# Dead tiles that hold evacuations and two more raw weight tiles, a quadrant joined by DMA, and a chunk's bank from another pool

## The chip, the cores and the metric

The kernel runs on one core of a Trainium2 chip. The metric is the device time of one execution in microseconds (us). TensorE is called PE, VectorE DVE, ScalarE ACT, GpSimd POOL, and SyncE SP; SP issues most of the weight loads and POOL the transfers that accumulate.

## What is computed

Two layers of a hybrid decoder on 512 tokens of width 1024, in float32, and a last norm:

```python
def hybrid_layer(x, ...):
    h = rmsnorm(x, g_mix)
    z = h @ w_in                       # q, k, v | retention q, k, v, g | two gates
    A = sliding_window_sink_attention(rope(aq), rope(ak), av, sinks) @ w_a
    B = (group_norm(chunkwise_retention(rq, rk, rv)) * silu(rg)) @ w_b
    x = x + (sigmoid(ga) * A + sigmoid(gb) * B) @ w_out
    return x + jnp.square(jax.nn.relu(rmsnorm(x, g_mlp) @ w_up)) @ w_down   # 1024 -> 4096 -> 1024

def reference(x, ...):
    for l in range(2): x = hybrid_layer(x, ...)
    return rmsnorm(x, g_final)
```

## The kernel before, in words

**Precision.** Every float32 product is made of three products of rounded halves: a weight `raw` is rounded by ACT into `hi` (L308), DVE takes the difference `lo` (L309), and `products` issues hi·hi, lo·hi and hi·lo as three matmuls (L354, L355, L356). A matmul has 512 or 256 columns.

**Weights.** They come as 361 units of 128 x 1024 in one order (`order`): per layer 46 of `w_in`, then `w_a`, `w_b`, `w_out`, and those of the MLP. `unit` hands out a unit's `hi` and `lo`; before that it splits up to unit i + SPLIT (3) and loads (`load_until`) up to AHEAD (4) units beyond that. There are 5 `raw` tiles and 4 each of `hi` and `lo`. A `raw` tile is given back when its unit is split, so a load, which SP issues, waits for an earlier unit's `lo` or add.

**The MLP** goes in 8 blocks e of 512 hidden columns. It saves products in the way of Strassen: a block's down part has seven products (`down`, parts 0 to 6 of the units "block") on four quadrants (i, j) of the output, i the half of the features and j the half of the tokens, and for e > 0 the up part is two "pair"s of four units each. Sums of weights are made beforehand by POOL DMAs into DRAM (`sum_steps`) or by DVE on the way: `add_part` (L267) for pair parts 1 and 2, `add_block` (L290) for block parts 2 and 4, which are the sum of two earlier raw tiles and load nothing while e < 7. Pair evacuations (`eu`, L1154, L1157; `z`, L1159, L1172; `mm`, L1152) make relu and the hidden forms, whose rounded halves `r` (L361, L362) PE multiplies with the block's units.

**Joining the output.** Blocks 0 to 6 (`Adding`): ACT copies twelve banks a block to SBUF, scaled (L1276), four `early` ones to temporaries `eu` and eight `put` ones to temporaries `y`, all from one pool of 7 buffers; a POOL DMA adds each to `y` in DRAM (L1278). Block 7 (`Ending`): POOL loads the four quadrants back (L1292), DVE adds the last products onto them (`add`, L1307), and the two `early` products of quadrant (1, 1) go by an ACT copy and an accumulating POOL DMA (L1302, L1303). In layer 0 `turn` then transposes each quadrant on PE (L1334) and DVE adds it to x (L1340); quadrants with i = 0 inside `last_but_one`, those with i = 1 in `carry`, which runs inside the first group of layer 1 (j = 1 first, then 0). `scaled_input` splits x into `xh` (L364) and `xl` (L365). In layer 1 the last norm follows instead: a gain product (L1316), squares on ACT, a scale per token (L1323 and L1326), and the output. Its last block's down part takes four `w_end` units.

**Banks.** `ps_mm` has 5 PSUM banks and `ps_aux` 3. `group` multiplies the first four units of `w_in` on four banks at once (key, value, two query columns); two `chunk`s follow, each with one bank of `ps_mm`. The keys are rotated by DVE from their bank (L570, L571) once the norm's scale is known. In the first part of the MLP in layer 1, `turn_x` transposes x on PE (L1069) for the copy that `Adding` starts from (L1071, L1072); after that x is dead until block 7 loads `y` into it. In layer 0 a tile `late_box[0]` waits for the same purpose.

**Order.** Each engine runs its instructions in the order that a scheduler gives them when the kernel is built; no order is written by hand but that of the calls. A change of pools and buffers therefore also moves instructions. SP and POOL issue their DMAs in order too.

## Time and profile before

| | us |
| --- | --- |
| median of three runs (lowest, highest) | 1501.16 (1500.49, 1502.59) |
| the profiled execution | 1501.42 |
| its span, from the first to the last instruction | 1499.7 |
| PE, DVE, ACT, POOL busy | 1471.8, 1044.3, 940.9, 239.7 |

The profile shows one execution. The groups of instructions give a line, an engine, the tile written and the tiles read, a count, the busy time and the mean length, and how long the engine was idle just before them and for whom. The waits list who waited for whom: total, times, longest. The timeline shows single instructions with start and length, and in brackets the idle time before one. The stretches give, for a piece of the span, the busy time of each engine, the clock that PE was granted (1.00 is full) and the share of the DMA engines' time. "DMA to landing" is the least, the median and the greatest time from the issue of a DMA to its last packet. A matmul's shown length reaches past the start of the next one; spacing between starts is what counts.

### The profile page before, as it was taken

To read this page: it belongs to the slowest core of one execution; us is meant where nothing else is said; L and a number is where in the kernel's file an instruction comes from. 1 tells how busy PE (TensorE), PEld (TensorE's weight loads), DVE (VectorE), ACT (ScalarE), POOL (GpSimd) and SP (SyncE) were. 2 spreads that over 40 slices of the span, in tenths; PEclk is the share of its full clock that TensorE was granted. 3 is DMA by queue.
4 is the path that set the end of the run, shared out by engine and by line. 5 is a ranking of instruction groups with operands and counts; after the bars stand their busy time and mean duration, and the time that the engine had idled before them with its cause. 6 is when DMAs were issued, how large, how long until landed. Compare 5 with 4: busy or idle time off the path is not lost.

```text
span 1499.7 us, 21303 instructions
## 1 busy us (share of the span) xinstructions
PE 1471.8 (98%) x7787; PEld 1265.7 (84%) x7787; DVE 1044.3 (70%) x1589; ACT 940.9 (63%) x1551; POOL 239.7 (16%) x334
## 2 busy tenths in 40 slices
PE   9999999999999999999999999999999999999997
PEld 7888888888889999998778888888888789888885
DVE  6878568654677777776977775677447677777665
ACT  7657355532568888887755563555325778877775
POOL 0101121101002222223001011111000212222230
PEclk9999999999999999999999999999999999999999
DMA  7654997668227888888836579876443488888883
GB/s 257 189 169 113 303 256 185 185 179 223 92 72 220 211 215 218 223 213 230 290 100 182 147 207 273 223 205 155 140 121 110 122 205 213 210 219 211 218 205 126
DMA packets 100472, 286.25 MB, mean 191 GB/s; under 512 B 11664, under 2 KB 11792, under 8 KB 96528
## 3 DMA queue, kind: packets, MB, share of 16 engines
q0 software_dynamic: 38832, 114.31, 36.3%
q1 hardware_dynamic: 60816, 169.27, 33.5%
q8 instruction: 61, 1.00, 0.3%
q10 hardware_dynamic: 720, 1.31, 0.2%
q14 instruction: 43, 0.35, 0.1%
HBM read 231.37 MB, written 113.77 MB: 230 GB/s over the span
## 4 chain that ended last, share of the span: by engine, by line
PE 87%; DMA 6%; ACT 3%; DVE 2%; issue 2%; DVEq 0%; ACTq 0%
PE mm L354 23%; PE mm L355 23%; PE mm L356 23%; DMA raw<-w_down_in 3%; DMA raw<-w_pair_in 2%; PE rv L354 2%; PE rv L356 2%; PE rv L355 2%; PE b L354 2%; PE b L355 2%; PE b L356 2%; DVE lo L309 1%; PE score L705 1%; ACT hi L308 1%; PE pT L670 1%
## 5 line engine op out<-in xcount | busy, mean ns | idle before, releaser
L308 ACT ACTIVATE hi<-raw 128x1024 fp32r<-128x1024 f32 (+1 forms) x363 | 369.8, 1020 | 324.4 <-PE mm L355 195.4
L309 DVE TENSOR_TENSOR lo<-raw,hi 128x1024 fp32r<-128x1024 f32 (+1 forms) x364 | 424.5, 1170 | 201.9 <-ACT hi L308 199.8
L354 PE MATMUL mm<-xh,hi 128*128 128x512 f32 (+1 forms) x1008 | 358.4, 359 | 14.4 <-ACT eu L1154 9.5
L355 PE MATMUL mm<-xl,hi 128*128 128x512 f32 (+1 forms) x1008 | 356.9, 356 | 0.0
L356 PE MATMUL mm<-xh,lo 128*128 128x512 f32 (+1 forms) x1008 | 356.2, 356 | 0.7 <-DVE lo L309 0.7
L354 PE MATMUL mm<-r,hi 128*128 128x256 f32 (+1 forms) x736 | 238.7, 324 | 0.5 <-ACT mm L1152 0.5
L356 PE MATMUL mm<-r,lo 128*128 128x256 f32 (+1 forms) x736 | 238.9, 325 | 0.0
L355 PE MATMUL mm<-r,hi 128*128 128x256 f32 (+1 forms) x736 | 238.8, 324 | 0.0
L354 PEld LDWEIGHTS mm<-xh,hi 128*128 128x128 f32 x1008 | 190.7, 189 | 44.2 <-ACT eu L1154 12.5
L356 PEld LDWEIGHTS mm<-xh,lo 128*128 128x128 f32 x1008 | 190.7, 189 | 26.2 <-DVE lo L309 0.9
L355 PEld LDWEIGHTS mm<-xl,hi 128*128 128x128 f32 x1008 | 191.0, 189 | 25.5 <-DVE xl L365 0.2
L354 PEld LDWEIGHTS mm<-r,hi 128*128 128x128 f32 x736 | 139.8, 190 | 13.7 <-ACT mm L1152 0.7
L355 PEld LDWEIGHTS mm<-r,hi 128*128 128x128 f32 x736 | 139.8, 190 | 13.1
L356 PEld LDWEIGHTS mm<-r,lo 128*128 128x128 f32 x736 | 139.8, 190 | 11.3
L1278 POOL DMA_DIRECT2D y<-eu x56 | 47.3, 851 | 387.7 <-ACT eu L1276 383.4
L1278 POOL DMA_DIRECT2D y<-y x112 | 98.1, 1257 | 66.4 <-DMA y<-eu 35.5
L355 PE MATMUL mm<-lo,r 128*128 128x512 f32 x272 | 104.2, 392 | 0.0
L356 PE MATMUL mm<-hi,r 128*128 128x512 f32 x272 | 100.7, 390 | 0.0
L354 PE MATMUL mm<-hi,r 128*128 128x512 f32 x272 | 97.8, 393 | 0.2
L267 DVE TENSOR_TENSOR raw<-raw 128x512 f32<-128x512 f32 x56 | 38.5, 688 | 67.6 <-DMA raw<-sums_up 54.1
L354 PE MATMUL b<-hi,r 128*128 128x512 f32 x180 | 70.5, 392 | 1.6 <-DVE y L1307 1.6
L355 PE MATMUL b<-lo,r 128*128 128x512 f32 x180 | 70.3, 390 | 0.0
(262 smaller groups left out, 2314.3 us busy)
## 6 DMA issues: line engine op xcount, KB each, us to landing
raw<-w_in_in SPq DMA_DIRECT2D x89, 512.0 KB, 5.5
sums_down<-w_down_in POOLq DMA_DIRECT2D x30, 1024.0 KB, 11.3
y<-y POOLq DMA_DIRECT2D x120, 256.0 KB, 7.9
sums_up<-w_pair_in POOLq DMA_DIRECT2D x56, 512.0 KB, 9.8
raw<-w_down_in SPq DMA_DIRECT2D x45, 512.0 KB, 8.7
raw<-w_pair_in SPq DMA_DIRECT2D x84, 256.0 KB, 4.2
raw<-sums_down SPq DMA_DIRECT2D x30, 512.0 KB, 9.1
y<-eu POOLq DMA_DIRECT2D x58, 256.0 KB, 5.8
```

What stands on the lines that cost most here:

```text
L267: nc.vector.tensor_tensor(raws[i][:, at], last[:, LEFT], last[:, RIGHT], ALU.add)
L308: nc.scalar.activation(hi[:, at], raw[:, at], AF.Copy)
L309: nc.vector.tensor_tensor(lo[:, at], raw[:, at], f32(hi[:, at]), ALU.subtract)
L354: nc.tensor.matmul(ps, ah, bh, start=start and i == 0, stop=False, **more)
L355: nc.tensor.matmul(ps, ah, bl, start=False, stop=False, **more)
L356: nc.tensor.matmul(ps, al, bh, start=False, stop=stop and i == n - 1, **more)
L670: nc.tensor.transpose(pt[:, i * P : (i + 1) * P], sm[:, at : at + P], ident)
L705: nc.tensor.matmul(ps[:, g * w : (g + 1) * w], q_s[g][:, c, at], part[:, keys], start=i == 0, stop=i == 1)
L1278: nc.gpsimd.dma_start(y[:, block, i * T : (i + 1) * T], t, **how)
```

## The change

1. `chunk` takes a pool; the last chunk of query columns in each layer takes its bank from `ps_aux`.
2. In layer 0's block 7 the `put` of quadrant (1, 1) is no longer added by DVE but copied by ACT and added by a POOL DMA, as its `early` products are; `carry` turns j = 0 first.
3. `Adding.put` uses a dead tile every second time: one of x's first four slices in layer 1, one of the waiting tile's in layer 0. There are four of them.
4. In layer 1, after the last `turn_x`, the upper half of x becomes two spare raw tiles, lent to pair and block units up to block 6 (`lent`); loads then run two units further ahead (`load_until`), and `fits` holds a load back while no tile of either kind is free.
5. In the last norm the gain product for i = 1 is joined with its scale into one DVE operation of three operands: four DVE instructions fewer.

```diff
--- before.py
+++ after.py
@@ -50,6 +50,7 @@
 DEEP = 3
 DELAY = 2
 AHEAD = 4
+RAW = 5
 SPLIT = 3
 
 
@@ -166,8 +167,22 @@
 
         return (slice(0, UNIT // 2), slice(UNIT // 2, UNIT)) if i < 3 else (slice(0, UNIT),)
 
-    def raw_tile():
-        return wpool.tile([P, UNIT], F32, tag="raw", name="raw", bufs=5)
+    spare = []
+
+    def lent(i):
+        if order[i][1] not in ("pair", "block") or block_of(order[i]) == N_BLOCK - 1:
+            return []
+        return [t for t in spare if not any(t is r for r in raws.values())]
+
+    def fits(i):
+        if order[i][1] == "block" and order[i][3] in (2, 4) and order[i][2] < N_BLOCK - 1:
+            return True
+        taken = sum(not any(t is r for t in spare) for r in raws.values())
+        return taken < RAW or bool(lent(i))
+
+    def raw_tile(i):
+        got = lent(i)
+        return got[0] if got else wpool.tile([P, UNIT], F32, tag="raw", name="raw", bufs=RAW)
 
     x_next = [1]
 
@@ -177,7 +192,7 @@
         nc.sync.dma_start(x[:, k, :], xT[:, k, :])
 
     def load_until(n):
-        while state["loaded"] < min(n, len(order)):
+        while state["loaded"] < min(n, len(order)) and fits(state["loaded"]):
             i = state["loaded"]
             layer, name, j = order[i][:3]
             if name == "pair":
@@ -185,7 +200,7 @@
             elif name == "block":
                 load_block(i)
             else:
-                raws[i] = raw_tile()
+                raws[i] = raw_tile(i)
                 for at in halves(i):
                     queue = nc.scalar if i == 0 and at.start == 0 else nc.sync
                     source = w_end[j] if name == "w_end" else weights[name][layer, j]
@@ -245,11 +260,14 @@
                 if next(steps[0], DONE) is DONE:
                     steps.pop(0)
 
+    def block_of(unit):
+        return unit[2] // 2 + 1 if unit[1] == "pair" else unit[2]
+
     def load_part(i):
         layer, _, j, part = order[i]
         source, sums = w_pair[layer, j], sums_up[layer][j]
         H = UNIT // 2
-        raws[i] = raw = raw_tile()
+        raws[i] = raw = raw_tile(i)
         if part == 0:
             nc.sync.dma_start(raw[:, LEFT], source[:, :H])
             nc.sync.dma_start(raw[:, RIGHT], sums[:, RIGHT])
@@ -270,7 +288,7 @@
         layer, _, e, part = order[i]
         if part in (2, 4) and e < N_BLOCK - 1:
             return
-        raws[i] = raw = raw_tile()
+        raws[i] = raw = raw_tile(i)
         if part in (2, 4):
             nc.sync.dma_start(raw, sums_last[:, part // 2 - 1, :])
             return
@@ -292,7 +310,7 @@
     def split_until(n):
         while state["split"] < min(n, len(order)):
             i = state["split"]
-            load_until(i + AHEAD)
+            load_until(i + AHEAD + len(spare))
             name, part = order[i][1], order[i][-1]
             if name == "pair":
                 add_part(i)
@@ -385,11 +403,11 @@
         while background:
             advance()
 
-    def chunk(name, layer, moving, evacuate, rate=1.0):
+    def chunk(name, layer, moving, evacuate, rate=1.0, pool=ps_mm):
 
         hi, lo = unit(name, layer)
         n = len(moving)
-        ps = bank(ps_mm, "mm")
+        ps = bank(pool, "mm")
         pairs = [((hi[:, k * P : (k + 1) * P], lo[:, k * P : (k + 1) * P]), moving[k]) for k in range(n)]
         advance(rate)
         products(ps, pairs[: n // 2], True, False)
@@ -650,7 +668,7 @@
             {0: squares, 1: rms_mix.prepare, 2: stats} if layer == 0 else {0: carried.pop(), 2: rms_mix.prepare, 3: stats},
         )
         chunk("w_in", layer, xs, put_q(2))
-        chunk("w_in", layer, xs, put_q(3))
+        chunk("w_in", layer, xs, put_q(3), pool=ps_aux)
         turn_v()
 
         a_t = [slots.four() for _ in range(2)]
@@ -1253,6 +1271,9 @@
                 into.put(1, 0, m, b[m], -1)
             into.end()
 
+        homes = [x[:, n, :] if last else late_box[0][:, n, :] for n in range(4)]
+        own = [0]
+
         class Adding:
 
 
@@ -1269,7 +1290,11 @@
                 self.send(i, j, m, temp("eu"), ps, sign, last or self.e > 0)
 
             def put(self, i, j, m, ps, sign):
-                self.send(i, j, m, temp("y"), ps, sign, last or self.e > 0 or j == 1)
+                self.send(i, j, m, self.home(), ps, sign, last or self.e > 0 or j == 1)
+
+            def home(self):
+                own[0] += 1
+                return homes[own[0] // 2 % 4] if own[0] % 2 else temp("y")
 
             def send(self, i, j, m, t, ps, sign, add):
                 block = 2 * j + m
@@ -1298,9 +1323,12 @@
                 if i == 0:
                     self.add(i, j, m, ps, scale)
                 else:
-                    t = temp("eu")
-                    nc.scalar.activation(t, ps, AF.Copy, scale=scale)
-                    nc.gpsimd.dma_start(self.y[i, j, m], t, accum_op=ALU.add)
+                    self.send(i, j, m, ps, scale)
+
+            def send(self, i, j, m, ps, scale):
+                t = temp("eu")
+                nc.scalar.activation(t, ps, AF.Copy, scale=scale)
+                nc.gpsimd.dma_start(self.y[i, j, m], t, accum_op=ALU.add)
 
             def add(self, i, j, m, ps, scale):
                 v = self.y[i, j, m]
@@ -1308,19 +1336,23 @@
 
             def put(self, i, j, m, ps, sign):
                 block = 2 * j + m
-                self.add(i, j, m, ps, (factor if sign > 0 else negative)[:, block : block + 1])
+                scale = (factor if sign > 0 else negative)[:, block : block + 1]
+                if not last and (i, j) == (1, 1):
+                    self.send(i, j, m, ps, scale)
+                else:
+                    self.add(i, j, m, ps, scale)
                 if last:
                     v = self.y[i, j, m]
                     first, total, both = (sq[:, n * NB + block : n * NB + block + 1] for n in range(3))
                     nc.scalar.activation(temp("junk"), v, AF.Square, accum_out=both if i else first)
-                    nc.vector.tensor_tensor(v, v, last_gain[:, i, :], ALU.mult)
                     if not i:
+                        nc.vector.tensor_tensor(v, v, last_gain[:, i, :], ALU.mult)
                         nc.vector.tensor_scalar(first, first, 1.0 / D, EPS, ALU.mult, ALU.add)
                         return
                     nc.scalar.activation(total, both, AF.Sqrt, bias=first, scale=1.0 / D)
                     nc.vector.reciprocal(total, total)
                     v = self.y[1, j, m]
-                    nc.vector.tensor_scalar(v, v, total, None, ALU.mult)
+                    nc.vector.scalar_tensor_tensor(v, v, total, last_gain[:, 1, :], ALU.mult, ALU.mult)
                     nc.sync.dma_start(out[:, block, T:], v)
                     v = self.y[0, j, m]
                     nc.scalar.activation(v, v, AF.Copy, scale=total)
@@ -1353,7 +1385,7 @@
 
             def carry(self):
                 for half in range(2):
-                    for j in (1, 0):
+                    for j in range(2):
                         self.turn(1, j, half, ps_aux)
                     for k in (4 + 2 * half, 5 + 2 * half):
                         scaled_input(k, g_mix + 2)
@@ -1376,6 +1408,7 @@
                     for n in range(KD):
                         turn_x(used[n % 2], n // 2, n % 2)
                     nc.scalar.activation(sq[:, 0:1], factor[:, 0:1], AF.Sqrt)
+                    spare.extend(x[:, a : a + 2, :].rearrange("p a t -> p (a t)") for a in (4, 6))
                 for ps in used:
                     nc.tensor.matmul(ps, ones, xh[:, 0, :], start=True, stop=True)
                 sum_input(2)
```

## The prediction, made before the result was known

> **What bounds the kernel now.** I read the busy times first, then who made TensorE (PE) wait, then the stretches around each wait, because an engine that is 98% busy can only gain where it stands still.
>
> ```profile
> span 1499.7 us, 21303 instructions
> PE 1471.8 (98%) x7787; PEld 1265.7 (84%) x7787; DVE 1044.3 (70%) x1589; ACT 940.9 (63%) x1551; POOL 239.7 (16%) x334
> ```
>
> PE is idle for 1499.7 − 1471.8 = 27.9 us. No edit takes a matmul away, so that sum, with matmuls slowed by the clock, is all there is to win. The waits of PE over the whole span:
>
> ```profile
> PE mm L354 <- ACT eu L1154: 9.5, 9, 2.0
> PE mm L354 <- DVE rot L570: 2.8, 1, 2.8
> ...
> L308 ACT ACTIVATE hi<-raw 128x1024 fp32r<-128x1024 f32 (+1 forms) x363 | 369.8, 1020 | 324.4 <-PE mm L355 195.4
> L309 DVE TENSOR_TENSOR lo<-raw,hi 128x1024 fp32r<-128x1024 f32 (+1 forms) x364 | 424.5, 1170 | 201.9 <-ACT hi L308 199.8
> ```
>
> (Total, times, longest; then, from the page's groups, the two halves of what every weight unit needs before PE can use it: ACT's rounding, 1.02 us, and DVE's difference, 1.17.) The other waits are between the layers, at the start and behind the last matmul. The profiled execution took 1501.42 us, 1.72 more than its span; the median of the three timed runs is 1501.16. I sum against 1501.42 and subtract 0.26 at the end. Two tenths of a per cent, which a measurement of this kernel can tell from no change, are 3.0 us.
>
> **The change part by part.**
>
> *The chunk's bank.* The last chunk of query columns in layer 1 stands at 770.5. The stretch before it ended, the hole, and what followed:
>
> ```profile
> 770.50:773.60 3.10, 0.35 (x2) 0.00 (x0) 2.99 (x4) 2.91 (x5) 0.00 (x0) 0.92 0.01 3
> 773.60:776.40 2.80, 2.73 (x6) 2.16 (x7) 2.80 (x6) 1.77 (x3) 0.00 (x0) 0.50 0.61 193
> ...
> 770.23 0.39 PE L355 MATMUL mm<-xl,hi 128*128 128x512 f32 x1
> 770.46 0.39 PE L356 MATMUL mm<-xh,lo 128*128 128x512 f32 x1
> 773.67 0.80 PE L354 MATMUL mm<-xh,hi 128*128 128x512 f32 x1 [2.83 <-DVE rot L570]
> ...
> 776.40 0.45 PE L354 MATMUL mm<-xh,hi 128*128 128x512 f32 x1
> ```
>
> The first two rows are stretches (length, PE, weight loads, DVE, ACT, POOL, granted clock, DMA share, GB/s), the others PE's timeline. PE waits 2.83 us until the rotation of the keys (L570) has read the `ps_mm` bank, and then runs six matmuls at a clock of 0.50: they take 776.40 − 773.67 = 2.73 where six at full speed take 6 x 0.23 = 1.38 (0.23 from 770.23 to 770.46). With a `ps_aux` bank neither is due: 2.83 + 1.35 = **4.2 gained**. The following chunk now takes the rotated bank, but PE gets there 24 matmuls (5.5 us) later, when L570 has long run. Bounds: 2 (the scores behind it wait for the same rotated keys) to 4.6.
>
> The Trainium skill ("TensorE: Matmul & The Clock Gate", Part 1: The HAM clock gate) puts the gate's fall at an idle window of about 3.4 us, free-running, and the way back at as much busy time. By that figure a 2.83 us hole need not have cooled the clock and the sum here would be 2.8; the trace shows 0.50 for 2.8 us, and I go by the trace.
>
> *Between the layers (702 to 745).* Four holes. Two come from ACT, which evacuates a gate late behind a weight's rounding; in the changed order the evacuations stand ahead of it. The others:
>
> ```profile
> PE mm L354 <- ACT eu L1154: 1.8, 1, 1.8
> PE mm L354 <- ACT mm L1152: 0.5, 1, 0.5
> ...
> 734.99 0.47 PE L354 MATMUL b<-hi,r 128*128 128x512 f32 x1 [1.57 <-DVE y L1307]
> ...
> 740.53 0.73 PE L354 MATMUL mm<-xh,hi 128*128 128x512 f32 x2 [1.32 <-ACT xh L364]
> ...
> L1303 POOL DMA_DIRECT2D y<-eu x2: 884/904/924, 723.3 to 724.5; - x2
> DMA to landing us min/median/max: 5.2/5.2/5.3
> ...
> DMA to landing us min/median/max: 6.4/8.4/12.4
> ```
>
> (Waits of the stretch 700 to 782, two rows of PE's timeline, then POOL's accumulating DMAs in 690 to 745: the early ones of the last block, L1303, with their landings, and the landings of the block before, L1278.) The first two holes, 2.3 us, I count as gained. The third goes too, since quadrant (1,1) is no longer added by DVE ahead of the bank's next use. In their place PE, which runs in order, now waits at the first turn of (1,1): a copy of some 0.7 (an estimate, from 1.02 for twice the columns), the issue of 0.9 and a landing of 5.2 make 6.8 us from the last matmul of that product, and the program has about 5 us of PE work in between (22 matmuls). That is a wait of 1.8. Behind that turn stand its DVE add, the adds of two more turns than before, the splitting of x, and the whole first group of layer 1, which already waited 1.32: I take 1.9 for that. 2.3 + 1.57 + 1.32 − 1.8 − 1.9 = **1.5 gained**, between −1.7 (landing 8.4) and +3.5 (the DMA hidden). At the slowest landing, 12.4, it would be −5.7.
>
> *Homes for the evacuations.* ACT's copies go to dead tiles every second time. They number the same and cost the same; ACT is 63% busy, and in layer 0 the order on DVE and PE is unchanged but for the end: **0** (±0.8). In layer 1 one such copy slips between the last turns that feed PE, 0.25 us.
>
> *Two more raw tiles, up to block 1.* They are the upper half of x, free only when the last turns of x have run. The raw loads of block 0's parts 5 and 6, issued in the old kernel near 1151 and 1156, now wait for that:
>
> ```profile
> 1188.65 0.51 PE L1380 MATMUL ssq<-xh,ones 128*128 128x512 f32 x1 [0.25 <-ACT y L1071]
> 1192.56 0.39 PE L354 MATMUL b<-hi,r 128*128 128x512 f32 x1
> ...
> DMA to landing us min/median/max: 3.4/3.8/4.2
> DMA to landing us min/median/max: 6.1/9.9/10.3
> ...
> 1199.06 0.39 PE L356 MATMUL mm<-xh,lo 128*128 128x256 f32 x1 [0.65 <-DVE lo L309]
> ...
> 1220.39 0.39 PE L354 MATMUL mm<-xh,hi 128*128 128x256 f32 x1 [1.95 <-ACT eu L1154]
> ```
>
> (PE's timeline; between, landings of the 512 KB loads of L284 in 1150 to 1160 and in 1205 to 1221.) The load can start at about 1188.5. PE wanted part 5 at 1192.6 in the old order and 12 matmuls (2.7 us) later in the new one, 1195.3. Landing after 6 us, 1194.5, and rounding and difference (2.2) behind it give 1196.7: **1.5 lost**, between 0 (3.4 us) and 5.7 (10.3). I take 6 because four accumulates, but only one other load of this size, run beside it. Against it the holes of 0.65 and 1.95 go, since their loads start earlier; block 1 loses about 0.8 by the ACT order told next. 2.6 − 0.25 − 1.5 − 0.8 = **0**.
>
> *Blocks 2 to 6.* What the old kernel loses there:
>
> ```profile
> PE mm L354 <- ACT eu L1154: 7.3, 7, 2.0
> ...
> 1299.41 1.06 ACT L308 ACTIVATE hi<-raw 128x1024 fp32r<-128x1024 f32 x1 [0.67 <-DMA raw<-w_down_in]
> 1300.38 0.36 ACT L1154 ACTIVATE eu<-mm 128x256 f32<-128x256 f32 x1
> ...
> 1300.79 0.39 PE L354 MATMUL mm<-xh,hi 128*128 128x256 f32 x1 [0.85 <-ACT eu L1154]
> ...
> 1464.01 0.39 PE L354 MATMUL mm<-xh,hi 128*128 128x256 f32 x1 [2.02 <-ACT eu L1154]
> ```
>
> (Waits of 1188 to 1490, then timelines of ACT and PE.) ACT waits for the load of a block's first part, and the evacuation that PE needs stands behind it. Of the 7.3 us, 1.95 was counted above and 2.02 belongs to the last block's `w_end`, whose load gets no lent tile: **3.3 gained**, as the load now starts a block part earlier.
>
> What is late next is the new order itself. In blocks 2 to 6 the scheduler now puts ACT's rounding of part 5 and one evacuation ahead of the copy of the sums that PE needs:
>
> ```profile
> 1270.76 0.63 ACT L361 ACTIVATE r<-sums 128x512 fp32r<-128x512 f32 x1
> 1271.28 1.06 ACT L308 ACTIVATE hi<-raw 128x1024 fp32r<-128x1024 f32 x1
> 1272.23 0.38 ACT L1172 ACTIVATE z<-mm 128x256 f32<-128x256 f32 x1
> ...
> 1271.85 0.39 PE L354 MATMUL b<-hi,r 128*128 128x512 f32 x1
> ...
> 1273.14 1.22 DVE L309 TENSOR_TENSOR lo<-raw,hi 128x1024 fp32r<-128x1024 f32 x1
> ...
> 1281.20 0.28 PE L356 MATMUL mm<-xh,lo 128*128 128x256 f32 x1
> ...
> DMA to landing us min/median/max: 3.9/5.5/7.0
> ```
>
> (ACT, PE, DVE, PE; the last row the landings of the pair loads of L257 in 1222 to 1463.) The copy (L361) ends at 1271.39 and PE uses it at 1271.85. Behind a rounding (0.95 to the next start) and an evacuation (0.3) it ends at 1272.6: **0.8 lost** in each of five blocks, 4.0. Then DVE: the two adds of the next pair now stand ahead of the difference that PE wants at 1281.20 + 0.8 = 1282.0, where they stood behind it. The second add needs a load that SP issues when part 5's difference (1273.14 + 1.2) is done: 1274.4 + landing + add 0.7 (an estimate: half the columns of a difference) + difference 1.2. That is 1282.0 at a landing of 5.7, so the median of 5.5 just fits and the slowest, 7.0, costs 1.3 a block. Block 2 alone has its first pair load a part later: 0.8. 3.3 − 4.0 − 0.8 = **1.5 lost**, from −8 to +3.3.
>
> *The tail.* Behind the last matmul DVE works without a pause:
>
> ```profile
> L1307 DVE SCALAR_TENSOR_TENSOR x<-mm,columns,x 128x512 f32<-128x512 f32 x8 | 5.7, 744 | 4.9 <-PE mm L356 4.9
> L1316 DVE TENSOR_TENSOR x<-x,late 128x512 f32<-128x512 f32 x8 | 5.4, 679 | 0.0
> L1323 DVE TENSOR_SCALAR x<-x,sq 128x512 f32<-128x512 f32 x4 | 1.9, 476 | 0.0
> ```
>
> Four gain products of 0.68 fall away; four scalings of 0.48 become products of three operands, which by L1307 take 0.74: 4 x 0.68 − 4 x 0.26 = 1.7 less on DVE. The last add of a bank stands behind most of it, but the last matmul bounds that add too, so 0.6 to 1.7 comes through: **1.0 gained**.
>
> Sum: 4.2 + 1.5 + 0 − 1.5 + 1.0 = 5.2, so 1501.42 − 5.2 = 1496.2 for an execution like the profiled one and, 0.26 less, **1496.0 us**.
>
> **The rivals.**
>
> 1. *The holes simply close.* No order costs anything and the accumulate is hidden: 4.2 + 3.5 + 2.4 + 3.3 + 1.0 = 14.4, 1486.8. For it: every hole of 1188 to 1463 but one names a late load. Against it: the order on ACT, which no load changes. 0.14.
>
> 2. *Slower: the pair adds hold DVE.* DVE works in order, and in blocks 2 to 5 an add that waits for its load now stands in front of a difference that PE wants. Each us of landing over 5.7 costs each of four blocks 1 us. From 7.75 the change is slower than before by 3.0 (8.2 us over four blocks); at the 9.9 of the crowded stretch above it is 4.2 x 4 = 16.8 worse, 1512.8. For it: two more tiles mean more transfers in flight. Against it: the slowest of those loads so far took 7.0, and they start ahead of the block's accumulates. 0.12.
>
> 3. *The loads for block 0 land late.* All transfers share the DMA engines, 10.3 us instead of 6: 4.2 more lost, 1500.2. The Trainium skill ("DMA: Bandwidth & Descriptors", Issuing engines are not separate DMA queues) says that DMAs of SP, ACT and POOL run on the same 16 engines and interleave; the two landing rows of L284 agree, 3.8 in a quiet stretch and 9.9 in a full one. 0.15.
>
> 4. *The chunk's wait does not go.* The scores behind it wait for the same keys and take the 4.2 back: 1500.2. Against it: between the hole and the first score lie two chunks. 0.09.
>
> **How the numbers follow.** The forecast has 0.50, with a range of its own of 1492 to 1500; a tenth of it lies within 0.2%. Faster by over 0.2% (under 1498.2): 0.44 of the forecast, 0.14 of the first rival, 0.05 of the third and fourth together, 0.63. Same: 0.06 + 0.19 = 0.25. Slower: the second rival, 0.12. The range that leaves out most of the first rival and of the second is 1489.5 to 1503.5.
>
> **What would show it.** In the changed profile: no hole ahead of the chunk near 768 and a clock of 1.00 there; a PE wait for a POOL DMA at the turn of (1,1), of 1 to 3 us; a wait of 0 to 3 us for part 5 of block 0, on the rounding or the difference; in blocks 2 to 6 one wait of 0.5 to 1 us for the copy of the sums and none for the gate's evacuation (L1154, L1172 after); `w_end`'s 2 us unchanged; a tail 1 us shorter. Waits of PE for a difference that come once per block and exceed 1 us would make the second rival right; a wait for the accumulate of over 5 us would undo the second step.

## The result, and the profile after

The changed kernel takes 1510.86 us (median of five runs, 1507.07 to 1512.86) where the kernel before takes 1501.16 (five runs, 1497.70 to 1503.12; the table ahead holds three of them): a ratio of 1.0064, 95% interval 1.0042 to 1.0085. It is slower, by some 9.7 us; 1496.0 was forecast, within 1489.5 to 1503.5. The profiled execution took 1509.6, its span 1507.8. From the page of the changed kernel:

```profile
span 1507.8 us, 21280 instructions
...
PE 1475.5 (98%) x7787; PEld 1268.2 (84%) x7787; DVE 1043.8 (69%) x1583; ACT 943.7 (63%) x1553; POOL 242.5 (16%) x336
```

PE stands still for 1507.8 − 1475.5 = 32.3 us, 4.4 more than before, and is busy 3.7 us longer with the same matmuls: part of the loss is clock. Who made PE wait, over the whole span (total, times, longest):

```profile
PE mm L374 <- DVE r L380: 8.2, 2, 4.4
PE turn L1366 <- DMA y<-eu: 3.9, 2, 2.8
PE mm L372 <- ACT eu L1172: 3.4, 5, 1.1
PE b L372 <- ACT r L379: 3.3, 5, 0.7
...
PE mm L373 <- DVE lo L327: 0.8, 1, 0.8
```

(Lines have moved: L1154 is L1172 now, L361 and L362 are L379 and L380, L309 is L327, L267 is L285, L1307 is L1335, L1334 is L1366.) The first row was not there before: twice PE waits over 3.7 us for the difference of a hidden form. The chunk's wait (2.8 for L570) is gone, and so are PE's waits for the gate's evacuations in layer 1, but for one of 1.1 ahead of the last block's `w_end`; the five waits of 0.65 for the copy of the sums, and the turn's waits for the accumulate, are those that the forecast described.

PE issues the same 7787 matmuls in both kernels. So the n-th matmul can be looked up in both traces; the later start minus the earlier one is the loss up to there, and its change over a stretch is what the stretch cost (single matmuls stand in another order here and there, which moves the difference by up to 0.4):

| stretch (us of before) | forecast | measured |
| --- | --- | --- |
| start to 702, layer 0's blocks | 0 | +2.0 |
| 702 to 745, between the layers | −1.5 | +2.5 |
| 745 to 1188, with the chunk | −4.2 | −4.4 |
| 1188 to 1221, block 0 of layer 1 | 0 up to block 1 | −2.8 |
| 1221 to 1262, block 1 | (in the row above) | +6.6 |
| 1262 to 1420, blocks 2 to 5 | +1.5 with block 6 | +0.4 |
| 1420 to 1450, block 6 | (in the row above) | +6.0 |
| 1450 to the last matmul | 0 | −1.3 |
| behind it | −1.0 | −0.9 |
| sum | −5.2 | +8.1 |

8.1 is the difference of the spans, 1507.8 − 1499.7. Two stretches hold 12.6 us of loss, and they are those of the two waits for L380. The stretches of the changed kernel around its waits (length, PE, weight loads, DVE, ACT, POOL, granted clock, DMA share, GB/s):

```profile
739.00:745.00 6.00, 3.16 (x13) 2.87 (x14) 4.89 (x8) 4.53 (x8) 0.00 (x0) 0.68 1.00 358
745.00:752.00 7.00, 7.00 (x27) 5.69 (x27) 7.00 (x12) 4.78 (x10) 0.00 (x0) 0.78 0.57 214
766.00:781.00 15.00, 15.00 (x68) 12.42 (x67) 10.52 (x15) 10.38 (x17) 0.00 (x0) 1.00 0.32 97
...
1221.60:1225.50 3.90, 0.14 (x2) 0.06 (x1) 1.41 (x3) 0.00 (x0) 0.00 (x0) 1.00 0.36 134
1225.50:1230.00 4.50, 4.50 (x13) 3.55 (x14) 4.50 (x7) 2.65 (x4) 0.00 (x0) 0.62 0.07 12
...
1433.40:1438.00 4.60, 4.54 (x13) 3.62 (x14) 4.60 (x8) 2.79 (x4) 0.00 (x0) 0.63 0.00 0
```

At the chunk (third row) PE is busy throughout at full clock. At 1221.6 it does nothing for 3.9 us, nor does ACT, and then runs 4.5 us at 0.62: 4.5 x 0.38 = 1.7 us more on top of the wait. The hole at 1429 is followed by 4.6 us at 0.63. What PE waits for shows in the timelines of SP, DVE and PE:

```profile
1213.57 0.42 SPq L273 DMA_DIRECT2D raw<-sums_up  x1
...
1216.51 1.23 DVE L327 TENSOR_TENSOR lo<-raw,hi 128x1024 fp32r<-128x1024 f32 x1 [0.26 <-ACT hi L326]
1224.09 0.69 DVE L285 TENSOR_TENSOR raw<-raw 128x512 f32<-128x512 f32 x1 [6.36 <-DMA raw<-sums_up]
1224.70 0.68 DVE L380 TENSOR_TENSOR r<-z,r 128x512 fp32r<-128x512 f32 x1
...
1225.44 0.50 PE L374 MATMUL mm<-hi,r 128*128 128x512 f32 x1 [3.76 <-DVE r L380]
...
1432.11 0.69 DVE L285 TENSOR_TENSOR raw<-raw 128x512 f32<-128x512 f32 x1 [7.04 <-DMA raw<-sums_up]
1432.72 0.68 DVE L380 TENSOR_TENSOR r<-z,r 128x512 fp32r<-128x512 f32 x1
```

DVE is idle for 6.36 us in front of a pair add whose raw tile has not landed. The add belongs to a weight that nobody needs yet; behind it in DVE's order stands the difference r (0.68 us), whose inputs are there (ACT, which makes one of them, has been idle since 1220.2), and PE needs that one. The same at 1432. The load was issued at 1213.57 and the add began at 1224.09, 10.5 us later. In the kernel before, SP's timeline has the same load 12 us later, behind the block's own loads:

```profile
1225.53 0.42 SPq L255 DMA_DIRECT2D raw<-sums_up  x1
```

In blocks 2 to 5 the same load is as late: issued at 1259.88, 1300.29, 1340.48 and 1380.67, it lands 9.6 to 9.8 us later. But there the add stands eight instructions further back, behind the differences r, and DVE comes to it 0.1 to 0.3 us after the landing. In block 2:

```profile
1263.97 0.68 DVE L380 TENSOR_TENSOR r<-z,r 128x512 fp32r<-128x512 f32 x1
...
1269.69 0.68 DVE L285 TENSOR_TENSOR x<-raw 128x512 f32<-128x512 f32 x1
```

What was on the way in 1205 to 1224 of the changed kernel (KB each, median us from issue to landing):

```profile
y<-y POOLq DMA_DIRECT2D x3, 256.0 KB, 11.7
...
raw<-w_down_in SPq DMA_DIRECT2D x1, 512.0 KB, 10.6
...
raw<-sums_up SPq DMA_DIRECT2D x1, 256.0 KB, 10.4
```

Between the layers PE's timeline shows two waits at the turn of quadrant (1, 1), and the two stretches at 739 and 745 above the clock that follows them:

```profile
739.01 0.33 PE L1366 MATMUL turn<-ident,y 128*128 128x128 f32 x1 [1.08 <-DMA y<-eu]
742.17 2.39 PE L1366 MATMUL turn<-ident,y 128*128 128x128 f32 x10 [2.83 <-DMA y<-eu]
```

In the tail the gain products number four, and the scalings are products of three operands (groups of 1485 to the end):

```profile
L1335 DVE SCALAR_TENSOR_TENSOR x<-mm,columns,x 128x512 f32<-128x512 f32 x8 | 5.6, 743 | 4.9 <-PE mm L374 4.9
...
L1355 DVE SCALAR_TENSOR_TENSOR x<-x,sq,late 128x512 f32<-128x512 f32 x4 | 2.9, 743 | 0.0
...
L1349 DVE TENSOR_TENSOR x<-x,late 128x512 f32<-128x512 f32 x4 | 2.7, 678 | 0.0
```

### The profile page after: what moved, and what is told of

Read it like the earlier page. It is cut to its first block, busy times and chain, and to the rows that moved or that the text cites. A ratio compares the mean times of both kernels' runs of the same rounds, so it can differ in the third digit from the quotient of the medians.

```text
span 1507.8 us, 21280 instructions
## 1 busy us (share of the span) xinstructions
PE 1475.5 (98%) x7787; PEld 1268.2 (84%) x7787; DVE 1043.8 (69%) x1583; ACT 943.7 (63%) x1553; POOL 242.5 (16%) x336
## 4 chain that ended last, share of the span: by engine, by line
PE 75%; DMA 11%; issue 9%; DVE 2%; ACT 1%; POOL 1%; POOLq 0%; ACTq 0%; SPq 0%; DVEq 0%
PE mm L372 20%; PE mm L373 19%; PE mm L374 19%; DMA y<-eu 3%; DMA y<-x 2%; DMA raw<-w_down_in 2%; PE rv L372 2%; PE rv L374 2%; PE rv L373 2%; PE b L372 1%; PE b L373 1%; PE b L374 1%; POOL y L1303 1%; DMA y<-y 1%; PE score L723 1%
## 5 line engine op out<-in xcount | busy, mean ns | idle before, releaser
L326 ACT ACTIVATE hi<-raw 128x1024 fp32r<-128x1024 f32 (+1 forms) x329 | 336.4, 1023 | 310.2 <-PE mm L373 205.3
L327 DVE TENSOR_TENSOR lo<-raw,hi 128x1024 fp32r<-128x1024 f32 (+1 forms) x330 | 385.9, 1174 | 199.6 <-ACT hi L326 196.9
L1303 POOL DMA_DIRECT2D y<-y x56 | 73.4, 1414 | 8.0 <-ACT x L1301 3.0
L374 PEld LDWEIGHTS mm<-hi,r 128*128 128x128 f32 x272 | 51.9, 191 | 20.2 <-DVE r L380 9.1
## 6 DMA issues: line engine op xcount, KB each, us to landing
sums_down<-w_down_in POOLq DMA_DIRECT2D x30, 1024.0 KB, 11.1
y<-y POOLq DMA_DIRECT2D x64, 256.0 KB, 10.5
```

The lines of the kernel that those rows point to most:

```text
L326: nc.scalar.activation(hi[:, at], raw[:, at], AF.Copy)
L327: nc.vector.tensor_tensor(lo[:, at], raw[:, at], f32(hi[:, at]), ALU.subtract)
L374: nc.tensor.matmul(ps, al, bh, start=False, stop=stop and i == n - 1, **more)
L1303: nc.gpsimd.dma_start(y[:, block, i * T : (i + 1) * T], t, **how)
```

## The experiments

**Theory:** the lent tiles let SP issue a pair's loads some 12 us earlier, into the crowd of a block's accumulates and weights; the load lands late, the pair add waits at the head of DVE's order, and r behind it. **Rivals:** the evacuations' homes or the quadrant by DMA move DVE's order; or the transfers are only slower altogether. Each ratio is to runs of the kernel before on the same chip, with its 95% interval. "Loss" is the difference of n-th matmuls.

### One part alone, one part less

`bank_only` and `bank_tail` are the kernel before with item 1, and with items 1 and 5:

```diff
-        ps = bank(ps_mm, "mm")
+        ps = bank(pool, "mm")
...
-        chunk("w_in", layer, xs, put_q(3))
+        chunk("w_in", layer, xs, put_q(3), pool=ps_aux)
```

> The chunk's bank alone, everything else as before. Theory: it is the one part that gives what was counted; the hole of 2.83 us and the half clock behind it go, so 4.2 us are gained (2 to 4.6), about 1497. Rival (the scores behind the chunk wait for the same keys): the time stays at 1501 and the hole is found again a chunk or two later.

> The chunk's bank and the joined gain product, nothing else. Both worked as forecast in the trace of the whole change (4.4 us at the chunk, 0.9 behind the last matmul), so 5.2 us are gained, 0.9965 of the time before; faster than the bank alone by 0.9. If the two do not add, the ratio is that of the bank alone, 0.9977.

Measured: `bank_only` 1496.77, 0.9977 (0.9964 to 0.9989), with 4.4 us gained between 766 and 781 and none given back by the scores; `bank_tail` 1495.58, 0.9963 (0.9946 to 0.9979). Both came out as expected: the chunk's term stands.

`spare_only` is the kernel before with item 4; `no_spare` the whole change without it; `no_homes` the whole change without item 3. The core of `no_spare`'s edit:

```diff
-            load_until(i + AHEAD + len(spare))
+            load_until(i + AHEAD)
...
-                    spare.extend(x[:, a : a + 2, :].rearrange("p a t -> p (a t)") for a in (4, 6))
```

> The two lent raw tiles alone. Theory (the order on DVE: a pair add that waits for its load stands ahead of the rounded sums that PE needs): waits of PE for DVE's r of 3 to 5 us in block 1 or 6, each followed by a piece at half clock, so 3 to 10 us slower than before, 1504 to 1511. Rival (the lent tiles hurt only together with the other parts, because homes let more accumulates go at once): 1497 to 1502.

> The whole change without the lent raw tiles. Theory (the lent tiles cost about 11 us by the two waits for r and what follows them, and give back about 3 in block 0): no wait of PE for r in blocks 1 and 6, 1498 to 1502. Rival (the accumulates from the homes and the joined quadrant are what is slow): the time stays at 1507 or above.

> The whole change without the homes. Theory (homes let accumulates leave earlier and crowd the loads, in layer 0 too, where PE has lost 2 us in four waits for the evacuation of L1172): the layer 0 waits go, 2 us, and the waits for r in blocks 1 and 6 shrink, 1503 to 1508. Rival (homes are neutral, as was forecast, and the layer 0 waits vary from run to run): 1509 to 1512, waits for r as long as before.

Measured: `spare_only` 1515.92, 1.0111 (1.0093 to 1.013); `no_spare` 1497.46, 0.9986 (0.9974 to 0.9997); `no_homes` 1512.13, 1.0088 (1.0071 to 1.0106). The lent tiles alone make the kernel slower (by more than the theory's 1504 to 1511), and without them the change is not. The homes do not bring the stalls, as the theory for `no_homes` had it: without them PE still waits 3.6 and 2.5 us for r, and block 1 and block 6 still cost 6.7 and 4.2 us (loss from 1221 to 1240: −1.92 to 4.81; from 1420 to 1435: 8.58 to 12.77).

### The add ahead of r

`pool_add`, the whole change with two of its adds, those that stood ahead of the two late differences, on GpSimd:

```diff
-            nc.vector.tensor_tensor(raws[i][:, at], last[:, LEFT], last[:, RIGHT], ALU.add)
+            (nc.gpsimd if order[i] in ((1, "pair", 2, 1), (1, "pair", 12, 1)) else nc.vector).tensor_tensor(raws[i][:, at], last[:, LEFT], last[:, RIGHT], ALU.add)
```

> The whole change, with the two pair adds that stand ahead of r on DVE (pair 2 and pair 12 of layer 1, part 1) made by POOL. The loads stay as they are. Theory (the place of the add in DVE's order costs the time): the waits of PE for r, 3.8 and 4.5 us, and the half clock behind them go, 10 to 13 us less than the change, 1496 to 1500, although these loads still land after some 10 us. Rival (the loads are late for everything): PE waits as long a little later, for the difference of these parts, and the time stays within 3 us of 1509.

Measured: 1496.57, 0.9979 (0.9968 to 0.999). PE's waits:

```profile
PE mm L372 <- ACT eu L1172: 3.6, 6, 0.8
PE b L372 <- ACT r L379: 2.5, 4, 0.6
PE turn L1366 <- DMA y<-eu: 2.3, 1, 2.3
PE mm L373 <- DVE lo L327: 1.3, 1, 1.3
```

The row for L380 is gone; 1.3 for a `lo` is what is late next. Two adds of 0.69 us on another engine are worth 1.0064 − 0.9979 = 0.85%, some 12.8 us. The two loads still land some 10 us after their issue, and yet 1221 to 1240 costs 1.7 us where the changed kernel loses 6.9, and 1420 to 1435 gains 0.9 where it loses 6.1. That the adds' place in DVE's order was the cause is shown.

`short_sums`, the whole change where the accumulates of blocks 1 to 6 of layer 1 carry a quarter of their columns (the rest of those sums is left out):

```diff
-                nc.gpsimd.dma_start(y[:, block, i * T : (i + 1) * T], t, **how)
+                c = P if last and self.e else T
+                nc.gpsimd.dma_start(y[:, block, i * T : i * T + c], t[:, :c], **how)
```

> The whole change, with the accumulating DMAs of blocks 1 to 6 of layer 1 cut to a quarter of their columns (three quarters of these sums are left out); the adds stand where they stood. Theory (the loads that the adds wait for take 10 us and not 5 because they run beside eight accumulates and four loads): they land in 5 to 7 us, the two waits for r fall from 8.2 us together to 0 to 3, 1497 to 1502. Rival (the loads take 10 us because there are seven raw tiles' loads in flight, accumulates or not): waits and time stay, 1507 to 1512.

Measured: 1501.54, 1.001 (0.9997 to 1.0022). Block 6's load, issued at the same place, now lands so (issues of 1415 to 1434):

```profile
raw<-sums_up SPq DMA_DIRECT2D x1, 256.0 KB, 4.0
y<-x POOLq DMA_DIRECT2D x1, 64.0 KB, 7.2
```

and of the two waits one is left:

```profile
PE mm L374 <- DVE r L380: 4.1, 1, 4.1
```

In the whole change that load took 11.1 us. Block 6's wait is gone; block 1's, whose loads run beside the accumulates of block 0, which are uncut, stands at 4.1 (the theory allowed 3 for both). The same kernel thus holds the case and its control: the late landing comes from the accumulates.

`lend_block0`: tiles lent only to block 0 of layer 1 and to the layer's first two pairs, and no quadrant by DMA:

```diff
-        if order[i][1] not in ("pair", "block") or block_of(order[i]) == N_BLOCK - 1:
+        if order[i][1] not in ("pair", "block") or block_of(order[i]) > 1 or order[i][1:3] == ("block", 1):
```

> Bank, homes and gain, with tiles lent only to block 0 of layer 1 and its first two pairs; no quadrant by DMA. Theory (the loads of later pairs then go out no earlier than in the kernel before, and the stall needs a load that is issued into a crowd of accumulates and weights): no wait for r of over 1 us at block 1 or block 6, and block 0 keeps what the lent tiles gave (3 us at 1221 us of before): 1492 to 1496, ratio 0.994 to 0.997. Rival (any lent tile that frees a raw tile early brings the stall): a wait of 3 to 5 us for r at the second group of block 1, 1499 to 1503, ratio 0.999 to 1.001.

Measured: 1499.65, 0.9987 (0.9976 to 0.9998). No wait for L380, as the theory has it; but the time missed its range, for a loss of 3.7 us between the layers that the next experiments explain. Block 0 gains 2.8 us, but not by the lent tiles, as the theory took for granted: `no_spare` gains 3.0 there without them, and `spare_only`, with them and without homes, 1.1.

### Between the layers: quadrant, homes, bank

`quad_only`, the kernel before with item 2; `quad_homes_tail`, the whole change without bank and lent tiles; `bank_homes_tail`, without quadrant and lent tiles. The quadrant's core:

```diff
-                self.add(i, j, m, ps, (factor if sign > 0 else negative)[:, block : block + 1])
+                scale = (factor if sign > 0 else negative)[:, block : block + 1]
+                if not last and (i, j) == (1, 1):
+                    self.send(i, j, m, ps, scale)
+                else:
+                    self.add(i, j, m, ps, scale)
```

> The joined quadrant alone. Theory (the turn waits for the accumulate's landing, and the clock is at half behind the wait of 2.8 us): PE is later by 2 to 3 us at the first group of layer 1 than before, 1502 to 1504. Rival (it gives 1.5 us, as was forecast): 1499 to 1500.

> The change without the chunk's bank and without the lent tiles. Theory (with the quadrant's order the chunk's hole is already gone, so that bank and quadrant share one gain): no gap of PE over 0.4 us at the chunk's first matmul, and a time within 0.5 us of the kernel with the bank (1497.5, ratio 0.9986). Rival (the terms add up, as the forecast summed them): the hole of the kernel before stands and the time is 4 to 4.6 us longer, 1502, ratio 1.0015.

> The change without the quadrant by DMA and without the lent tiles: chunk's bank, homes and fused gain. Theory (homes cost about 2 us in layer 0 and give about 3 us in block 0 of layer 1; the bank gives 4.4 us on its own and the fused gain about 1.5): PE at 702 us of before about 2 us later than in the kernel with bank and gain alone, at 1221 us about 1 us earlier than it, end 0 to 1.5 us earlier: 1494 to 1496, a ratio of 0.995 to 0.9965. Rival (the homes are a loss that only the quadrant or the lent tiles made good): 1 to 2 us later than bank and gain alone, 1496.5 to 1498, a ratio of 0.997 to 0.998.

Measured: `quad_only` 1499.46, 0.9989 (0.9977 to 1.0001); `quad_homes_tail` 1496.07, 0.9965 (0.9951 to 0.9979); `bank_homes_tail` 1499.81, 0.9989 (0.9976 to 1.0001). In `quad_only` PE loses 4.6 us from 702 to 745 (702: 1.90, 745: 6.52), and its waits of 700 to 790 are

```profile
PE turn L1341 <- DMA y<-eu: 3.6, 2, 2.5
PE mm L354 <- ACT eu L1154: 1.8, 1, 1.8
PE mm L354 <- ACT mm L1152: 0.5, 1, 0.5
```

so neither the first holes go nor is the accumulate hidden. The time is nevertheless the rival's, because 4.3 us come back at the chunk, whose hole is gone without the bank:

```profile
773.35 0.39 PE L543 MATMUL ssq<-sh,ones 128*128 128x512 f32 x1
773.58 0.39 PE L354 MATMUL mm<-xh,hi 128*128 128x512 f32 x1
...
774.03 0.39 PE L543 MATMUL ssq<-sl,ones 128*128 128x512 f32 x1
...
775.09 1.23 DVE L561 TENSOR_TENSOR tab<-rawtab,rstd 128x1024 f32<-128x1024 f32 x1 [1.49 <-ACT rstd L544]
776.35 0.69 DVE L570 TENSOR_TENSOR rot<-mm,tab 128x512 f32<-128x512 f32 x1
777.21 0.45 PE L354 MATMUL mm<-xh,hi 128*128 128x512 f32 x1
```

In the order that the quadrant brings, the norm's sums of squares (L543) stand nine matmuls earlier ahead of the chunk and DVE's next `lo` ahead of the table (L561), so L570 has read the bank when PE comes to it at 777.21. `quad_homes_tail` confirms it: no hole at the chunk, and 4.3 us gained from 766 to 781 without the bank. Bank and quadrant close the same hole; the rival, that the terms add up, falls. (That it came out below `no_spare` rather than level was not expected; the intervals touch.)

The theory for `bank_homes_tail` fell: homes cost more than they give, 0.9989 against 0.9963 for `bank_tail` (the intervals just meet), and more than the rival said. It loses 3.1 us from 702 to 745 although it has no quadrant by DMA. POOL's loads back (L1292 before, L1299 here) and DVE's wait, first before:

```profile
698.48 0.76 POOL L1292 DMA_DIRECT2D late<-y  x1 [0.64 <-PE mm L355]
702.61 0.74 POOL L1292 DMA_DIRECT2D late<-y  x1 [3.37 <-DMA y<-y]
```

Then `bank_homes_tail`, timeline and waits:

```profile
706.36 0.76 POOL L1299 DMA_DIRECT2D late<-y  x1 [6.20 <-DVE lo L309]
718.06 0.76 POOL L1299 DMA_DIRECT2D late<-y  x1 [4.17 <-DMA y<-late]
```

```profile
DVE late L1314 <- DMA late<-y: 1.9, 1, 1.9
```

The waiting tile is a home in layer 0, and it is also where block 7 loads two quadrants back. The second load goes out 15.5 us later, behind an accumulate that still reads the tile, and DVE, which is busy without a pause from 730 on, waits 1.9 us for it at the worst place. (2.5 in the changed kernel.)

`homes_but6` takes the homes from block 6 of layer 0 alone; `homes_l1` from all of layer 0:

```diff
-                return homes[own[0] // 2 % 4] if own[0] % 2 else temp("y")
+                return homes[own[0] // 2 % 4] if own[0] % 2 and (last or self.e < N_BLOCK - 2) else temp("y")
...
-                return homes[own[0] // 2 % 4] if own[0] % 2 else temp("y")
+                return homes[own[0] // 2 % 4] if last and own[0] % 2 else temp("y")
```

> Bank, homes and gain, but the last block that accumulates in layer 0 (block 6) uses no home. Theory (the waiting tile is lent as a home and is also where block 7's two quadrants are loaded back, so that its loads wait for the last accumulates that read it, and DVE for them): the loads back of the waiting tile go out near 698 and 702 again instead of 706 and 718, DVE waits for none of them, and PE at 745 us of before is within 1.5 us of the kernel without homes (2 for block 6's own stalls). End 1494 to 1496.5, ratio 0.995 to 0.997. Rival (the joint between the layers is late because the accumulates land late in the crowd): DVE still waits 1.5 us or more for a load back, and PE is 4 us or more late at 745 us.

> Bank, homes in layer 1 alone, and gain. Theory (homes cost only in layer 0, about 2 us in its blocks and 3 to 5 between the layers, and give about 1 us in layer 1): PE up to 1188 us of before as in the kernel with bank and gain alone (4.6 us earlier than before), 1 us earlier than it behind block 0; 1494 to 1495.5, ratio 0.9955 to 0.9965. Rival (the gain in layer 1 is only what PE had lost before it): the same as bank and gain alone from block 0 on, ratio 0.996 to 0.997, or slower.

Measured: `homes_but6` 1497.07, 0.9977 (0.9968 to 0.9986); `homes_l1` 1493.63, 0.9952 (0.9936 to 0.9967), the lowest median of all, though its interval overlaps `bank_tail`'s, and faster than both kernels. The loads back in `homes_but6`:

```profile
700.50 0.75 POOL L1299 DMA_DIRECT2D late<-y  x1 [0.68 <-PE mm L356]
704.54 0.74 POOL L1299 DMA_DIRECT2D late<-y  x1 [3.29 <-DMA y<-y]
```

DVE waits for no load back, and the stretch costs 1.2 us instead of 3.1 (702: 2.03, 745: 3.24); the time, for the 2.0 lost before it, missed its range by little. Three kernels with block 6's homes and without the quadrant lose 3.1 to 4.0 there, six with neither 0.0 to 1.3: block 6's homes were the cause, shown. `homes_l1` did not come to 1188 as early as `bank_tail` (−2.4, not −4.6), but gains 3.1 in block 0 of layer 1, where `bank_tail` gains 1.9.

### What is left without the stalls

`pool_add_noquad` is `pool_add` without item 2; `pool_add_but6` is `pool_add` with the homes of `homes_but6`; `pool_add_l1` is `pool_add_noquad` with homes in layer 1 alone. Their edits are the ones shown.

> Bank, homes, lent tiles and gain, with the two pair adds ahead of r's difference on GpSimd, and no quadrant by DMA. Theory (the two stalls are all that the lent tiles cost, and the quadrant by DMA costs its waits between the layers, 2.5 to 5 us, for a hole that the bank closes by itself): 2 to 5 us under the kernel with the quadrant (1496.6), so 1491.5 to 1494.5, ratio 0.9945 to 0.9965. Rival (the quadrant's waits only move idle time that comes anyway): within 1 us of it, ratio 0.9975 to 0.9985.

> The whole change with the two pair adds ahead of r's difference on GpSimd and no homes in block 6 of layer 0. Theory (both costs removed, and the quadrant by DMA stays): no wait of DVE for a load back, the turn's waits for the accumulate stay at 2 to 4 us; 1 to 3 us under the kernel with the adds on GpSimd alone (0.9979), a ratio of 0.996 to 0.9973. Rival (the turn waits for the accumulate anyway, and the load back was hidden behind that): within 0.5 us of it, a ratio of 0.9976 to 0.9982.

> Bank, homes in layer 1 alone, lent tiles, gain, and the two pair adds on GpSimd; no quadrant by DMA. Theory (what is left are the parts that give, each without its price): up to 1188 us of before 4.6 us earlier than before, behind block 0 as in the whole change another 2.9, end 7 to 9 us earlier than before; 1491 to 1495, ratio 0.994 to 0.9965. Rival (the lent tiles need the homes of layer 0 or cost elsewhere): not under bank and gain alone (0.9963) by more than 0.3 us, or slower.

Measured: 1500.18, 0.9988 (0.9976 to 1.0); 1500.98, 1.0002 (0.9988 to 1.0015); 1495.96, 0.9972 (0.996 to 0.9984). All three theories fell. The second one's rival fell too, the first one's was missed by little, and the third one's held. Without the quadrant DVE waits 2.7 us for the load back and the stretch costs 4.0; with the quadrant and without block 6's homes, the turn still waits 1.22 and 2.78 for the accumulate, the holes of 0.46 and 1.80 are back, and it costs 4.3. So either part alone costs 2.5 to 4.6 us there (six kernels), and both together −0.1 to 2.5 (five kernels with the same code there); part of both spreads is the clock, told at the end. Each closes holes that the other leaves: the ACT holes of 0.46 and 1.80 stand in all ten kernels without block 6's homes and in none of the eight with them.

`pool_add_l1`, free of both costs, is not faster than `homes_l1`. From 1188 to 1490 PE waits 6.0 us in `homes_l1`, all of it for the gate's evacuations; in `pool_add_l1` 1.2 of that is left, but 2.6 for the copy of the sums and 2.2 for `lo` have come in its place. The lent tiles give nothing here even without the two stalls.

## Why the prediction was wrong

The step that failed is the one that says what two more raw tiles cost behind block 0 ("Two more raw tiles, up to block 1" and "Blocks 2 to 6"). It gave no price to the first add of a pair, whose load is issued earlier too. In blocks 1 and 6 that add stands ahead of an r that PE needs, its load takes 10.4 and 11.1 us, and the two stretches lose 12.6 us. Step by step:

- **The chunk's bank** (4.2 forecast, 4.4 measured): right, with the half clock in it. The fourth rival, that the scores take it back, did not come about. Wrong was only that I added it to the quadrant's term: the quadrant's order closes the same hole.
- **Between the layers** (1.5 gained forecast, 2.5 lost): this step failed too. The first two holes went, but by the homes of block 6, which I had put at 0, and not by the quadrant. The turn waits for the accumulate as forecast, but for 1.08 and 2.83 instead of 1.8. In all PE stands still here for as long as before (0.67 + 0.60 + 1.08 + 2.83 = 5.2 us; before 0.46 + 1.80 + 1.57 + 1.32 = 5.2), and what is lost is the clock behind the long hole (0.68, then 0.78), which was not in the sum, though the trace of before had priced a 2.83 us hole at the chunk. And the step did not see the load back of item 3's tile. (By its own terms a hidden accumulate would have given 1.5 + 1.8 = 3.3, not 3.5.)
- **Homes for the evacuations** (0 forecast): failed. In layer 0 ten kernels with homes lose 2.0 to 4.4 us from 440 to 702 and seven without lose −0.1 to 0.9. Why is open: the 512 KB loads of a block (L284) land later there, with a median of 10.6 to 11.0 us from 500 to 700 in each of the ten and of 8.9 to 9.1 in the others, but no run separated that from ACT's order. In block 0 of layer 1 kernels with homes gain 1.6 to 3.2 us and those without 0.6 to 1.9. "They number the same and cost the same" was true of ACT's copies and beside the point: what a tile is lent for delays who owns it next.
- **Two more raw tiles, up to block 1** (0 forecast): the gain came, but not for the reason given. The two holes in block 0 closed (2.8 gained, of 2.6 forecast) and the feared 1.5 for part 5 did not come (its sum, 1196.7 − 1195.3, makes 1.4). But five kernels with homes in layer 1 and without lent tiles gain as much there (1.6 to 3.2), and two with lent tiles and without homes only 1.1 and 0.6. Then block 1: 6.6 lost.
- **Blocks 2 to 6** (1.5 lost forecast): blocks 2 to 5 came to 0.4, the five waits for the copy of the sums at 0.65 each where I had 0.8. Block 6 lost 6.0. This is the step that decides: the second rival's mechanism (an add that waits for its load holds DVE in front of what PE wants) is what happened, but I placed it in blocks 2 to 5 ahead of a `lo`, for the second add of a pair, and priced it at a landing of 5.5, the median of loads issued behind the crowd. In blocks 1 and 6 the first add stands ahead of r (L380), and its load, issued earlier, lands in 10.4 and 11.1 us. I said "they start ahead of the block's accumulates"; they start in the middle of the last block's. That blocks 2 to 5 came out near the forecast is luck: there the load lands 0.1 to 0.3 us before DVE reaches the add. Why the scheduler set the add ahead of r in blocks 1 and 6 alone is open.
- **The tail** (1.0 forecast, 0.9 measured): right. `w_end`'s wait, forecast unchanged, shrank from 2.0 to 1.1.

Without the two stalls (12.8 us by `pool_add`) the change would be some 3 us faster than before. That this is near the forecast's 5.2 is partly luck: 2.8 gained in block 0 and 1.3 ahead of the tail stand against 4.5 lost in layer 0 and between the layers, and the sum had none of the three.

## What to carry to other kernels

A tile that lets loads start earlier changes which transfers they run among: price the landing at the new issue time, not by the median of the old. Before giving an engine work that waits for a transfer, list what stands behind it in that engine's order; two adds moved to an engine with time to spare were worth 12.8 us. A dead tile is free only until its next owner: look up who writes it next and when, and lend it in the blocks that are far from that.

## What was unexpected of the hardware

A 256 KB load took 11.1 us among full accumulates of 256 KB and 4.0 at the same place among accumulates cut to 64 KB, though SP issues the one and POOL the others. The Trainium skill ("DMA: Bandwidth & Descriptors", Issuing engines are not separate DMA queues) says that DMAs of SP, ACT and POOL run on the same 16 engines and interleave; the trace agrees, with these two numbers.

Before, the holes of 1.57 and 1.32 us ahead of layer 1's first group left the clock at 1.00 (stretches of the kernel before):

```profile
739.00:745.00 6.00, 4.68 (x26) 3.73 (x25) 6.00 (x10) 6.00 (x11) 0.00 (x0) 1.00 0.94 328
745.00:752.00 7.00, 7.00 (x32) 5.80 (x31) 7.00 (x11) 4.89 (x9) 0.00 (x0) 1.00 0.45 170
```

In the changed kernel 1.08 and 2.83 behind each other were followed by 0.68 and 0.78, and 3.76 and 4.45 by 0.62 and 0.63 for some 4.5 us, which adds some 1.7 us to each of these two. These are means over stretches that hold both clocks; a shorter stretch behind the 2.83 is at half clock throughout:

```profile
742.20:747.00 4.80, 4.80 (x19) 4.31 (x20) 3.73 (x6) 4.80 (x10) 0.00 (x0) 0.50 0.96 344
```

In the 18 traces, start and tail aside, all 20 holes of 2.26 us and more were followed by 0.50, for 3.4 us or, behind two holes in a row, mostly for 6.8; none of the holes under 1.80 brought it by itself. In between a hole's length does not settle it. The hole of 1.80 us ahead of 712 stands in ten traces: in six 0.50 follows for 3.4 us, in four it does not. The stretches behind it in the kernel before and in `homes_l1`:

```profile
712.60:716.00 3.40, 3.38 (x23) 3.09 (x24) 3.40 (x6) 3.37 (x6) 0.00 (x0) 1.00 1.04 352
714.70:718.00 3.30, 3.30 (x13) 2.85 (x12) 3.30 (x7) 2.99 (x7) 0.74 (x1) 0.50 1.03 408
```

No run shows why. So one trace can lose 1.3 to 1.5 us more than another behind the same hole (713 to 716). That is all of the 1.2 that `homes_l1` and `homes_but6` lose between the layers. In the same way the spread from −0.1 to 2.5 with quadrant and homes is mostly clock: the two lowest have 3.4 us at half clock there and the three others 6.8.
